# Decoder step on one core: the first pair of each down-projection part by seven products, with weight sums made ahead and kept in DRAM

## The chip, the cores and the metric

The kernel runs on one core of one Trainium2 chip. The metric is the device time of one execution in microseconds (us), given as the median of the runs; lower is better. Engines are named as in the profile: PE (matrix products), DVE (elementwise work), ACT (copies, casts, activations), POOL (elementwise work and its own DMA queue) and SP (which only issues DMAs). The profile is one execution taken by the hardware profiler.

## What is computed

One layer of a decoder for 512 prompt tokens and 8 sample tokens (520 columns), D = 2048, feed-forward width 5632, in float32:

```
h = h + W_out [ GatedDeltaNet(x_n) ; MultiScalePool(x_n) ]    x_n = RMSNorm(h)
gu = RMSNorm(h) @ w_gate_up                                   # 2048 -> 2 x 5632
h = h + (silu(gu[..., :D_FF]) * gu[..., D_FF:]) @ w_down      # 5632 -> 2048
y = RMSNorm(h)
```

Only the last two products, gate/up and down, matter for this change. The result must hold to float32 accuracy, so that every operand is cut into a high part `hi` (float32r, a rounded copy) and a rest `lo` = x - hi, and a product of two 128-row tiles is three matmuls: hi x hi, hi x lo, lo x hi.

## The kernel before, in words

**Pairs and products.** The work of gate/up and down is tiled in pairs (class `Pair`): a pair makes two 128-row output tiles for all 520 columns. Its weight is a 2 x 2 block matrix (A11, A12, A21, A22: two output tiles by two halves of the contraction), its input a 2 x 2 block matrix (B11, B21 for the first 260 columns, B12, B22 for the last 260). Each block product is 8 tiles of the contraction deep in gate/up, and 7, 7 or 8 in down; each depth is three matmuls of 260 columns (`passes`, L1265 to L1270). Done plainly a pair takes eight block products (`plain`, L1324). Most pairs go by Strassen's scheme in the form of Winograd (`strassen`, L1401): seven products M1 to M7, on the weights A11, A12, A22 and four sums S1 to S4 of them, and on the inputs B11, B21, B22 and four sums T1 to T4. The sums of the inputs are shared by all pairs of a stage; the sums of the weights are made anew for each pair (`add`, L1284, one DVE operation each) and then cut (`cut_raw`: an ACT cast to hi at L1261, a DVE subtraction to lo at L1262).

**Look-ahead.** In `strassen` a weight is added up or cut three to four products before PE reads it. Three rotating buffers (`wpl`) and one extra take the cut weights in turn, so that a cut waits for the product four places earlier. Products go into five PSUM banks; `combine` (L1307) empties them on DVE, most of it after M6.

**Parts of down.** The contraction of down (44 tiles) is done in three parts (`SIZES = (7, 7, 8)` pairs of tiles). The inputs of a part are the eight quarters that gate/up wrote to DRAM (`a_d`, by `to_dram` on POOL). At the start of a part all seven forms (B11, B21, B22, T1 to T4, each with a hi and a lo tile in SBUF) change over while PE goes on: `cross` runs the last pair of the part before by eight plain products, then the first pair of the new part by eight plain products too, because plain pairs read only B11, B21, T1 and B22. In between, `fill` brings each form in: `fetch` loads it from `a_d` in pieces of two tiles into staging rows (POOL's DMA queue; free rows in the first part, seven rotating `st` buffers later), ACT cuts it to hi (L1831) and DVE to lo (L1832). The order of all this is written by hand in the tables `TAIL`, `LAST` and `HEAD`, whose entries are carried out at fixed steps of the two plain pairs. There are three such crossings, one for each part.

**Queues.** Weights are loaded by SP (L1253), forms and rows of h by POOL, each in program order. In gate/up a hook (`hidden`) is called ahead of each product and places other work there: the gating of each tile pair, and the recurrent state of the sample tokens (on POOL).

## Time and profile before

| | |
|---|---|
| median of 3 runs (lowest to highest) | 2152.28 us (2151.39 to 2152.33) |
| the profiled execution, its own time | 2151.82 us |
| its span | 2150.1 us |
| mean granted PE clock | 0.999 |
| PE busy | 2123.7 us, 17746 matmuls |
| DVE busy | 1757.6 us, 2629 instructions |
| ACT busy | 929.3 us |
| POOL busy | 490.9 us |
| moved by DMA | 305.44 MB |

Times in the profile are counted from the start of the span. A group line gives line, engine, operation, output and inputs, shape and count; then the busy time of the group in us and the mean of one in ns; then the idle time of its engine just ahead of it and who ended it. A timeline row gives start, duration, engine, line, operation, and in brackets the idle time ahead of it with its releaser. The window view gives for each stretch its length, the busy time of each engine with the count of its instructions, the granted PE clock, the share of time that the 16 DMA engines were busy, and the GB/s that they moved.

Gate/up's Strassen pairs run from about 820 to 1650 us, the three crossings lie near 1650, 1800 and 1945 us, and the span ends with the output stage from 2130 us.

### The profile page before, as it was taken

The numbers are of one execution on the slowest core, as the hardware profiler recorded it, in microseconds if no ns is written. First come the engines' busy times: TensorE is split into PE (matmuls) and PEld (weight loads), VectorE is DVE, ScalarE is ACT, GpSimd is POOL, SyncE is SP. The second block draws the span as 40 slices with busy tenths as digits, with TensorE's granted clock in tenths as the row PEclk, the third lists the DMA queues.
The fourth block names the chain that finished last, engine by engine and source line by source line (L and its number), as shares of the span: only waits on it lengthen the run. The fifth ranks groups of instructions, "written<-read, shape, count | busy, mean of one in ns | idle before, by whom it ended". The sixth has DMA issues, their size and how long they took to land.

```text
span 2150.1 us, 43041 instructions
## 1 busy us (share of the span) xinstructions
PE 2123.7 (99%) x17746; PEld 2110.5 (98%) x17746; DVE 1757.6 (82%) x2629; ACT 929.3 (43%) x1404; POOL 490.9 (23%) x602
## 2 busy tenths in 40 slices
PE   8999999999999999999999999999999999999998
PEld 7999999999999999999999999999999999999998
DVE  7786767666599979988888888888887897887997
ACT  6533442433255454434434434434434444435444
POOL 3212320222012202333333333331113302003100
PEclk9999999999999999999999999999999999999999
DMA  8344434434445534455455455454456746438333
GB/s 282 90 119 114 117 104 113 116 111 107 129 134 160 158 99 132 144 163 148 141 165 148 138 168 148 135 171 134 119 148 197 226 112 205 115 104 250 91 108 119
DMA packets 445826, 305.44 MB, mean 142 GB/s; under 512 B 27836, under 2 KB 424533, under 8 KB 442285
## 3 DMA queue, kind: packets, MB, share of 16 engines
q1 hardware_dynamic: 422733, 219.94, 36.6%
q0 software_dynamic: 21584, 81.95, 12.0%
q8 instruction: 139, 2.28, 0.4%
q10 hardware_dynamic: 1312, 0.80, 0.1%
q14 instruction: 58, 0.48, 0.1%
HBM read 255.66 MB, written 47.63 MB: 141 GB/s over the span
## 4 chain that ended last, share of the span: by engine, by line
PE 85%; DVE 8%; DMA 2%; issue 2%; ACT 1%; POOL 1%; DVEq 0%; SPq 0%; ACTq 0%; POOLq 0%
PE dn L1269 21%; PE dn L1268 21%; PE dn L1270 21%; PE mm L168 5%; PE mm L170 5%; PE mm L169 5%; DVE lo L1262 1%; DVE lo L137 1%; PE dn L870 1%; DMA st<-a_d 1%; DMA qk<-tok_d 1%; PE mm L1268 1%; PE mm L1269 0%; DVE raw L1290 0%; PE mm L1270 0%
## 5 line engine op out<-in xcount | busy, mean ns | idle before, releaser
L1262 DVE TENSOR_TENSOR lo<-raw,hi 128x1024 fp32r<-128x1024 f32 (+1 forms) x422 | 530.6, 1277 | 87.0 <-ACT hi L1261 85.5
L1261 ACT CAST hi<-raw 128x1024 fp32r<-128x1024 f32 (+1 forms) x422 | 427.5, 1027 | 403.1 <-DVE raw L1290 205.4
L168 PE MATMUL mm<-xh,hi 128*128 128x256 f32 (+1 forms) x1280 | 376.4, 294 | 3.1 <-DVE mixa L259 3.1
L169 PE MATMUL mm<-xl,hi 128*128 128x256 f32 (+1 forms) x1280 | 361.6, 283 | 0.9 <-DVE xl L350 0.7
L170 PE MATMUL mm<-xh,lo 128*128 128x256 f32 (+1 forms) x1280 | 361.7, 283 | 0.4 <-DVE lo L137 0.4
L168 PEld LDWEIGHTS mm<-xh,hi 128*128 128x128 f32 x1280 | 241.2, 188 | 7.1 <-DVE mixa L259 3.8
L169 PEld LDWEIGHTS mm<-xl,hi 128*128 128x128 f32 x1280 | 241.6, 189 | 1.7 <-DVE xl L350 1.7
L170 PEld LDWEIGHTS mm<-xh,lo 128*128 128x128 f32 x1280 | 240.9, 188 | 0.6 <-DVE lo L137 0.6
L1290 DVE TENSOR_TENSOR raw<-raw 128x1024 f32<-128x1024 f32 (+1 forms) x130 | 175.1, 1347 | 2.2
L1269 PE MATMUL dn<-b21l,hi 128*128 128x260 f32 x620 | 175.7, 283 | 0.1
L1270 PE MATMUL dn<-b21h,lo 128*128 128x260 f32 x620 | 175.4, 283 | 0.0
L1268 PE MATMUL dn<-b21h,hi 128*128 128x260 f32 x620 | 174.9, 282 | 0.0
L1270 PE MATMUL dn<-b11h,lo 128*128 128x260 f32 x612 | 173.2, 283 | 1.3 <-DVE lo L1262 1.3
L1269 PE MATMUL dn<-b11l,hi 128*128 128x260 f32 x612 | 173.3, 283 | 0.0
L1268 PE MATMUL dn<-b11h,hi 128*128 128x260 f32 x612 | 172.8, 282 | 0.0
L1454 POOL TENSOR_TENSOR mixa<-mixa 128x520 f32<-128x520 f32 x22 | 51.3, 2333 | 493.0 <-DVE mixa L1448 493.0
L1268 PE MATMUL dn<-T1h,hi 128*128 128x260 f32 x556 | 158.1, 284 | 0.0
L1269 PE MATMUL dn<-T1l,hi 128*128 128x260 f32 x556 | 157.7, 284 | 0.0
L1270 PE MATMUL dn<-T1h,lo 128*128 128x260 f32 x556 | 156.8, 282 | 0.0
L1268 PE MATMUL dn<-B22h,hi 128*128 128x260 f32 x548 | 155.9, 284 | 0.0
L1269 PE MATMUL dn<-B22l,hi 128*128 128x260 f32 x548 | 155.6, 284 | 0.0
L1270 PE MATMUL dn<-B22h,lo 128*128 128x260 f32 x548 | 154.6, 282 | 0.4 <-DVE lo L1262 0.4
(669 smaller groups left out, 6480.7 us busy)
## 6 DMA issues: line engine op xcount, KB each, us to landing
raw<-in_w_gate_up_dram SPq DMA_DIRECT2D x134, 512.0 KB
raw<-in_w_in_dram SPq DMA_DIRECT2D x79, 512.0 KB
a_d<-mixa POOLq DMA_DIRECT2D x22, 1040.0 KB, 5.5
raw<-in_w_down_dram SPq DMA_DIRECT2D x48, 448.0 KB
mixb<-in_w_gate_up_dram SPq DMA_DIRECT2D x41, 512.0 KB
raw<-in_w_out_dram SPq DMA_DIRECT2D x25, 512.0 KB
st<-a_d POOLq DMA_DIRECT2D x49, 260.0 KB, 6.6
raw<-in_w_down_dram SPq DMA_DIRECT2D x24, 512.0 KB
```

What stands on the lines that cost most here:

```text
L137: dve.tensor_tensor(lo[:, r], raw[:, r], hi[:, r].bitcast(F32), op=ALU.subtract)
L168: te.matmul(acc[ci], wh, hi[k][:, c0:c1], start=(k == 0), stop=False)
L169: te.matmul(acc[ci], wh, lo[k][:, c0:c1], start=False, stop=False)
L170: te.matmul(acc[ci], wl, hi[k][:, c0:c1], start=False, stop=(k == len(w) - 1))
L870: te.matmul(yp[0:96, c, j], xt_[:, c, :], udf[:, c, j] if it == 0 else v3(cur)[:, c, j], start=True, stop=True)
L1261: act.copy(hi, raw)
L1262: dve.tensor_tensor(lo, raw, hi.bitcast(F32), op=ALU.subtract)
L1268: te.matmul(acc, wh[:, k, :], xf[:, k, :], start=start and k == 0, stop=False)
L1269: te.matmul(acc, wh[:, k, :], xg[:, k, :], start=False, stop=False)
L1270: te.matmul(acc, wl[:, k, :], xf[:, k, :], start=False, stop=stop and k == wh.shape[1] - 1)
L1290: dve.tensor_tensor(r[name], r[a], r[b], op=op)
L1454: pool.tensor_tensor(q[:, 4:8:2, :], q[:, 1:4:2, :], q[:, 0:2, :], op=ALU.subtract)
```

## The change

The first pair of each part of down is computed by the seven products instead of eight. Its weight sums S1 to S4, cut into hi and lo, are made during gate/up and stored to DRAM (`sums_d`); at the crossing they are loaded back as they are. The forms are loaded straight into their own lo tiles and cut in place there, so that the staging rows go. For each of the three first pairs:

- in gate/up, `sums_ahead` is a generator of twelve steps, taken one per gate/up pair (ahead of product 5 of even pairs and of product 2 of odd ones): four loads of weight blocks, four sums and four lo cuts on DVE, four hi casts on ACT, and eight stores by SP;
- at the crossing, `recall` loads the eight tiles (SP), S1 to `xcp`, S2 to the pool "sg", S3 and S4 to the pool "sf"; A11, A12 and A22 are loaded and cut as before;
- the first pair's products go in the order `CROSSED`, and it joins the run of the other pairs of its part.

```diff
+    CROSSED = ("M4", "M7", "M1", "M6", "M5", "M2", "M3")
...
-    rows = [mix[m] for m in (4, 5, 10, 11, 12, 13, 14, 15)]
+    sums_d = dram.tile([len(SIZES), 4, 2, P, HG * P], F32, name="sums_d")
...
+        def recall(self, name, pool_):
+
+            src, n = self.sums[int(name[1]) - 1], self.width
+            w = [pool_.tile([P, HG * P], F32R, tag=x, name=x)[:, :n] for x in ("hi", "lo")]
+            for j, t in enumerate(w):
+                sp.dma_start(t.bitcast(F32), src[j, :, :n])
+            self.w[name] = [t.rearrange("p (k c) -> p k c", c=P) for t in w]
...
-        steps = [(q, n) for q in range(len(pairs)) for n in (order if q == len(pairs) - 1 else STEADY)]
+        steps = [(q, n) for q in range(len(pairs)) for n in (
+            CROSSED if pairs[q].sums is not None else order if q == len(pairs) - 1 else STEADY)]
...
+            if p4 and p4.sums is not None and name4[0] == "S":
+                name4 = ""
+            if p and p.sums is not None and name[0] == "S":
+                name = ""
...
     def fetch(name, part_):
 
-        n = SIZES[part_]
-        staged[name] = []
+        n, fp = SIZES[part_], sum(SIZES[:part_])
         for r in range(0, n, 2):
             k = min(2, n - r)
-            if part_ == 0:
-                st = rows[len(spare) % len(rows)]
-                spare.append(name)
-            else:
-                st = stage[-1][1].tile([P, NTOK], F32, tag="st", name="st", bufs=7)
...
+            pool.dma_start(forms[name][1][:, r:r + k, :].bitcast(F32),
+                           a_d[fp + r:fp + r + k, :, QUARTER.index(name), :].rearrange("k p c -> p k c"))
 
     def fill(name, part_):
...
         hi, lo = forms[name]
...
+        for r in range(0, SIZES[part_], 2):
+            x = slice(r, min(r + 2, SIZES[part_]))
+            raw = lo[:, x, :].bitcast(F32)
+            act.copy(hi[:, x, :], raw)
+            dve.tensor_tensor(lo[:, x, :], raw, hi[:, x, :].bitcast(F32), op=ALU.subtract)
...
-    LAST = {0: ("+A11", "+A21", "+A12", "T3"), 1: ("+A22", "B11"), 2: ("A11",), 3: ("T1", "A21"), 4: ("A12", "B21", "<B22")}
-    HEAD = {0: ("B22", "+A11", "+A22", "+A21"), 1: ("+A12",), 2: ("A11", "S3", "T2"), 3: ("A22",), 4: ("-S3", "S2")}
+    LAST = {0: ("<B11", "T3"), 1: ("+A12", "?S1"), 2: ("<T1", "A22", "T2"), 3: ("<B21", "A11", "B11"), 4: ("<B22", "T1")}
+    CROSS = {2: ("?S4", "B21"), 3: ("B22",)}
...
-    def cross(part_, last, done=None, then=None):
-
-        r21, r21_ = r21s if part_ == 0 else r21s[1:] * 2
+    def cross(part_, last):
+
+        first = dps[part_][0]
+        for x in ("T4", "T3", "T2"):
+            fetch(x, part_)
         last.cut("A12")
-        fill("T4", part_)
-        last.plain(lambda step: turn(LAST[step], dps[part_][0], r21, part_))
...
-        dps[part_][0].plain(lambda step: turn(HEAD[step], dps[part_][1], r21_, part_))
...
+        turn(("+A22", "?S3", "+A11", "?S2", "T4"), first, part_)
+        last.plain(lambda step: turn(LAST[step], first, part_))
...
     def hidden(q, j):
...
+        if j == (1 if q % 2 else 4):
+            next(ahead, None)
...
-        run(dps[part_ - 1][1:-1], r21s[1], None, STEADY, dps[part_ - 1][-1])
+        run(dps[part_ - 1][:-1], r21s[1], None, STEADY, dps[part_ - 1][-1], part_ - 1)
         cross(part_, dps[part_ - 1][-1])
```

In these tables `+` loads a weight block, `?` recalls a stored sum, `<` only fetches a form, a weight's bare name cuts it, and a form's bare name fills it. `LAST` is read at steps of the plain last pair (step 0 stands behind product 2, 1 behind 4, 2 behind 5, 3 behind 7, 4 behind 8), `CROSS` ahead of products 3 and 4 of the first pair.

**DVE in gate/up**, from the first sum of M6 of an early gate pair on, before:

```order
L1313 TENSOR_TENSOR cm<-cm,dn 128x260
L1314 TENSOR_TENSOR cm<-cm,dn 128x260
L1434 TENSOR_TENSOR sg<-cm,dn 128x260
L1262 TENSOR_TENSOR lo<-raw,hi 128x1024 x2
L1434 TENSOR_TENSOR sg<-cm,dn 128x260
```

and now, where L1262 has become L1263, L1313 and L1314 are L1323 and L1324, the gate's sums are L1451, and L1962 is a sum of `sums_ahead`:

```order
L1323 TENSOR_TENSOR cm<-cm,dn 128x260
L1324 TENSOR_TENSOR cm<-cm,dn 128x260
L1451 TENSOR_TENSOR sg<-cm,dn 128x260
L1263 TENSOR_TENSOR lo<-raw,hi 128x1024
L1962 TENSOR_TENSOR mixb<-mixb 128x896
L1263 TENSOR_TENSOR lo<-raw,hi 128x1024
```

One sum has come in between the cut of this pair's S4 and that of the next pair's A11, which stood next to each other.

**SP at the first crossing**, from the first load of a down weight, before (the number behind a name tells one buffer from another; the blocks are A11, A21, A12 and A22 of the first pair, then A11, A22, A21 and A12 of the second, and A21 of the third):

```order
L1253 DMA raw_19774<-in_w_down_dram 128x7x128
L1253 DMA mixb_99<-in_w_down_dram 128x7x128
L1253 DMA raw_19777<-in_w_down_dram 128x7x128
L1253 DMA raw_19845<-in_w_down_dram 128x7x128
L1253 DMA raw_20056<-in_w_down_dram 128x7x128
L1253 DMA raw_20058<-in_w_down_dram 128x7x128
L1253 DMA sg_9697<-in_w_down_dram 128x7x128
L1253 DMA raw_20109<-in_w_down_dram 128x7x128
L1253 DMA sg_9697<-in_w_down_dram 128x7x128
```

and now (A22; S3; A11; S2; A12; S1; A21 of the second pair; S4):

```order
L1254 DMA raw_19796<-in_w_down_dram 128x7x128
L1291 DMA hi_19798<-sums_d_7807 128x896
L1291 DMA lo_19799<-sums_d_7807 128x896
L1254 DMA raw_19802<-in_w_down_dram 128x7x128
L1291 DMA hi_19804<-sums_d_7807 128x896
L1291 DMA lo_19805<-sums_d_7807 128x896
L1254 DMA raw_19935<-in_w_down_dram 128x7x128
L1291 DMA hi_19937<-sums_d_7807 128x896
L1291 DMA lo_19938<-sums_d_7807 128x896
L1254 DMA sg_9698<-in_w_down_dram 128x7x128
L1291 DMA hi_20150<-sums_d_7807 128x896
L1291 DMA lo_20151<-sums_d_7807 128x896
```

Eight loads of stored sums have come in between the weight loads. The last two, S4, stand ahead of the loads of the second pair's A11, A22 and A12.

**DVE at the second crossing**, from the cut of the first pair's A12 on, before (`st` is a staging row, `b21` the tile of B21; L1867 and L1868 add a product to a row of h, the last plain product of the old part):

```order
L1262 TENSOR_TENSOR lo<-raw,hi 128x896
L1832 TENSOR_TENSOR b21l<-st,b21h 128x520 x3
L1832 TENSOR_TENSOR b21l<-st,b21h 128x260
L1867 TENSOR_TENSOR mixa<-mixa,cm 128x260
L1868 TENSOR_TENSOR mixa<-mixa,dn 128x260
L1832 TENSOR_TENSOR B22l<-st,B22h 128x520 x3
```

and now, from the fill of T1 to that of B21 (L1839 is L1832, L1874 and L1875 are L1867 and L1868):

```order
L1839 TENSOR_TENSOR T1l<-T1l,T1h 128x520 x3
L1839 TENSOR_TENSOR T1l<-T1l,T1h 128x260
L1874 TENSOR_TENSOR mixa<-mixa,cm 128x260
L1875 TENSOR_TENSOR mixa<-mixa,dn 128x260
L1839 TENSOR_TENSOR b21l<-b21l,b21h 128x520 x3
L1839 TENSOR_TENSOR b21l<-b21l,b21h 128x260
```

The adds of the last plain product stood between the fills of B21 and B22; now they stand right behind the fill of T1 and ahead of that of B21, and each fill reads the form's own lo tile.

124 lines of the change are left out of this document (85 added, 39 removed).

## Prediction

> **What bounds the kernel now.** I read the page first, then the stretches between, then single rows.
>
> ```profile
> span 2150.1 us, 43041 instructions
> ...
> PE 2123.7 (99%) x17746; PEld 2110.5 (98%) x17746; DVE 1757.6 (82%) x2629; ACT 929.3 (43%) x1404; POOL 490.9 (23%) x602
> ...
> PE 85%; DVE 8%; DMA 2%; issue 2%; ACT 1%; POOL 1%; DVEq 0%; SPq 0%; ACTq 0%; POOLq 0%
> ```
>
> PE is busy nearly all of the span, and the chain that ended last runs through PE for 85% of it. An average does not say where; the stretches that the change touches do:
>
> ```profile
> core 0: us, PE busy (x) PEld busy (x) DVE busy (x) ACT busy (x) POOL busy (x), PEclk, DMA share, GB/s
> 900.00:1000.00 100.00, 100.00 (x833) 100.00 (x832) 85.87 (x91) 39.48 (x49) 33.23 (x26) 1.00 0.50 148
> 1400.00:1500.00 100.00, 100.00 (x833) 100.00 (x832) 85.71 (x93) 41.28 (x52) 26.38 (x21) 1.00 0.51 150
> 1799.00:1841.00 42.00, 42.00 (x352) 42.00 (x351) 32.53 (x55) 23.97 (x41) 17.92 (x27) 1.00 0.84 254
> 1990.00:2130.00 140.00, 140.00 (x1165) 140.00 (x1164) 129.77 (x165) 69.14 (x84) 10.92 (x7) 1.00 0.33 91
> ```
>
> In gate/up (first two), in the second crossing (third) and in the last part of down (fourth) PE is never idle, at full clock. So a matmul taken out of these stretches shortens the span by its pace, if nothing new makes PE wait. DVE is the engine next to full, with 14 of 100 us free in gate/up. In the crossing it is DMA, at 0.84.
>
> The pace of a matmul is not the duration of its record. It comes from DVE's first sum after M6, which waits for PE in each pair:
>
> ```profile
> 1219.81 0.43 DVE L1313 TENSOR_TENSOR cm<-cm,dn 128x260 f32<-128x260 f32 x1 [1.12 <-PE dn L1270]
> ...
> 1240.04 0.42 DVE L1313 TENSOR_TENSOR cm<-cm,dn 128x260 f32<-128x260 f32 x1 [1.29 <-PE dn L1270]
> ...
> 1777.65 0.43 DVE L1313 TENSOR_TENSOR cm<-cm,dn 128x260 f32<-128x260 f32 x1 [1.64 <-PE dn L1270]
> ...
> 1795.34 0.43 DVE L1313 TENSOR_TENSOR cm<-cm,dn 128x260 f32<-128x260 f32 x1 [1.64 <-PE dn L1270]
> ```
>
> A pair of gate/up is seven products of 8 x 3 matmuls: 20.23 us / 168 = 0.1204 us. A pair of a seven-tile part of down is 17.69 us / 147 = 0.1203 us. So a product takes 2.53 us in parts one and two, and 2.89 us in part three and in gate/up.
>
> **The change, part by part: the product.** Each first pair loses one product of eight: 21 + 21 + 24 = 66 matmuls, 66 x 0.1204 = 7.95 us off PE. Taken by the record's mean
>
> ```profile
> L1268 PE MATMUL dn<-b21h,hi 128*128 128x260 f32 x620 | 174.9, 282 | 0.0
> ```
>
> it would be 66 x 0.282 = 18.6 us; but the records overlap (833 in 100 us), so that figure is no saving. The Trainium skill ("TensorE: Matmul & The Clock Gate", the section "Wait — 56ns, not 53.3ns?") gives a warm matmul N / 2.4 GHz plus about 2.5 ns, an estimate of 0.111 us for 260 columns and of 7.3 us for the 66. The trace's pace is 8% slower than that; the measured one is used.
>
> **Sums in gate/up.** Twenty-four DVE operations are added in 36 pairs: per part four sums and four lo cuts, one to a pair at most. The nearest rows for their kinds:
>
> ```profile
> L1290 DVE TENSOR_TENSOR raw<-raw 128x1024 f32<-128x1024 f32 (+1 forms) x130 | 175.1, 1347 | 2.2
> L1262 DVE TENSOR_TENSOR lo<-raw,hi 128x1024 fp32r<-128x1024 f32 (+1 forms) x422 | 530.6, 1277 | 87.0 <-ACT hi L1261 85.5
> L1290 DVE TENSOR_TENSOR sg<-raw,sg 128x896 f32<-128x896 f32 (+1 forms) x18 | 20.3, 1129 | 0.0
> L1262 DVE TENSOR_TENSOR lo<-sg,hi 128x896 fp32r<-128x896 f32 (+1 forms) x25 | 28.5, 1141 | 3.0 <-ACT hi L1261 2.6
> ```
>
> 16 of 896 columns at 1.13 and 8 of 1024 at 1.31 make 28.6 us of DVE over 36 x 20.23 = 728 us. That raises DVE from 86% to 90% there. What counts is whether one operation of 1.1 to 1.3 us makes a cut late:
>
> ```profile
> 1017.54 0.43 DVE L1313 TENSOR_TENSOR cm<-cm,dn 128x260 f32<-128x260 f32 x1 [0.20 <-PE dn L1270]
> ...
> 1221.13 2.35 DVE L1262 TENSOR_TENSOR lo<-raw,hi 128x1024 fp32r<-128x1024 f32 x2
> ```
>
> The second row is the cut of S4 and of the next pair's A11, done at 1223.48. M6 ended just ahead of 1219.81, and A11 is read after M5, M2 and M3, three products or 8.67 us later: a margin of 5.0 us, of which the inserted sum takes 1.1. S4 itself is cut ahead of it, at 1222.3, and read two products (5.78 us) after M6: a margin of 3.3 us, untouched. The lead is won back by the wait for M6, 1.1 to 1.3 us in the pairs shown ahead and 0.20 in the first row here, the shortest once the lead is built up. So I take the cost as nothing, with two covers: the margin of 3 to 5 us and then the wait. Without the covers it is 28.6 us. The twelve casts go to ACT, 40% busy there, and read sums finished a pair earlier. The twelve loads and 24 stores by SP (17.3 MB over 728 us, 24 GB/s on 148) take their inputs from the pair before, so SP does not stop in front of its weight loads for long.
>
> At the start of gate/up's pairs DVE is behind already, and the first sum falls there (ahead of the second pair's product 2):
>
> ```profile
> 841.27 0.39 PE L1270 MATMUL dn<-B22h,lo 128*128 128x260 f32 x1 [0.43 <-DVE lo L1262]
> ...
> 850.24 5.43 DVE L1262 TENSOR_TENSOR lo<-raw,hi 128x1024 fp32r<-128x1024 f32 x3
> ```
>
> PE idled 0.43 us for DVE at 841, and three cuts took 5.43 us a little later. One operation of 1.13 us here may cost PE from 0 to 1.1 us; I take 0.3, nearer to nothing, since from 900 us on PE does not stop.
>
> **The crossings.** Per crossing 8 x 448 KB of sums come back by SP in place of one block, 3.2 MB more (3.7 in the last). DVE's work hardly changes: one cut less, three adds of 0.42 us more. What is new is that a form can be loaded only when PE is done with its tile, where staging rows let the loads run ahead. T4, T3 and T2 are free before the plain pair begins. T1 is the tight one, because the adds of the last plain product stand behind its fill on DVE, and M6 of the first pair needs the PSUM bank that they empty:
>
> ```profile
> L1822 POOL DMA_DIRECT2D st<-a_d x56: 579/707/727, 1798.0 to 1979.0; - x56
> ...
> L1831 ACT CAST T1h<-st x8: 410/622/632, 1819.0 to 1969.2; 128x520 fp32r<-128x520 f32 x7, 128x260 fp32r<-128x260 f32 x1
> L1832 DVE TENSOR_TENSOR T1l<-st,T1h x8: 423/694/702, 1820.7 to 1969.9; 128x520 fp32r<-128x520 f32 x7, 128x260 fp32r<-128x260 f32 x1
> ...
> DMA to landing us min/median/max: 4.2/6.5/8.5
> ...
> L1867 DVE TENSOR_TENSOR mixa<-mixa,cm 128x260 f32<-128x260 f32 x44 | 18.6, 424 | 0.3
> L1868 DVE TENSOR_TENSOR mixa<-mixa,dn 128x260 f32<-128x260 f32 x44 | 18.7, 425 | 3.3 <-PE dn L1270 0.4
> ```
>
> Counted from the start of the second crossing's plain pair: T1 is free after five products, 12.6 us; four issues of 0.71 bring it to 15.5; landing takes 6.5 (at worst 8.5); the last piece is cast and subtracted in 0.83, the two adds take 0.85: 23.7 (25.7). M6 starts after eleven products, at 27.8. The margin is 4.1 (2.1) us, and more in the other two crossings, where products take longer. Behind a fetch that waits stand only the next fetches on POOL's queue; behind a cast that waits for its landing stand, on ACT, the casts of B21 and of the second pair, and on DVE their subtractions.
>
> S4's buffer is that of S3, so SP waits for M7, ten products or 25.3 us after the start, and behind SP's wait stand the second pair's A11, A22 and A12. M3 reads S4 at 35.4: 10.1 us for 2 x 448 KB. The nearest rows are three weight loads of 512 KB in gate/up:
>
> ```profile
> 1216.32 6.42 SPq L1253 DMA_DIRECT2D raw<-in_w_gate_up_dram  x3
> ...
> 1223.04 1.05 ACT L1261 CAST hi<-raw 128x1024 fp32r<-128x1024 f32 x1 [1.56 <-DMA raw<-in_w_gate_up_dram]
> ```
>
> The second had landed 6.7 us after the first was issued, with DMA at 0.5; that leaves 3.4 us. A11, 448 KB behind S4, lands some 2 to 3 us later and is wanted 15 products after the start, 37.9 us. I take 0.2 us for each crossing, 0.6 in all; the bounds are below.
>
> One wait at the third crossing goes with the old order:
>
> ```profile
> 1975.20 0.28 PE L1268 MATMUL dn<-b21h,hi 128*128 128x260 f32 x1
> 1975.54 0.39 PE L1269 MATMUL dn<-b21l,hi 128*128 128x260 f32 x1
> ```
>
> The step is 0.34 in place of 0.12: B21's fill came late by 0.2 us, as the first pair's third product. Now B21 is read by the sixth, so 0.2 us is gained. The tail keeps its order.
>
> **The sum.** -7.95 - 0.2 + 0.3 + 0.6 = -7.25 us on the profiled execution (2151.82 us; 1.72 outside the span): 2144.6. The median of the runs, 2152.28, is 0.46 above it: 2145.0.
>
> **The rivals.**
> *The crossings give some back.* Traffic of 42 us x 254 GB/s = 10.7 MB plus 3.2 is 13.9 MB in 39.5 us, where 254 / 0.84 = 302 GB/s at a full share move 11.9. The surplus of 2.0 MB is 6.5 us a crossing, if all lands within it; but T4, T3 and T2 (2.8 MB) are fetched during the Strassen pair ahead, which brings it to 11.1 MB, just below. So the bounds are 0 and 6.5 us; at 1 to 4 us each in place of 0.2, 2147.4 to 2156.4. For it speaks the thin rest, against it the margins of 2 to 4 us above. The Trainium skill ("DMA: Bandwidth & Descriptors", the section "Specifications") puts one core's share of memory at about 358 GB/s; by that 14.1 MB would fit and nothing be lost, but the rows' 302 is used.
> *Slower: the crossings are full.* Were the surplus paid whole, three times 6.5 is 19.5 us in place of my 0.6, and the time 2163.9. It turns slower than before from 2.6 us a crossing on (7.95 + 0.2 - 0.3 = 7.85, by three).
> *DVE falls behind in gate/up.* If the waits for M6 are no true spare, part of the 28.6 us shows on PE: 0.2 us in each of the 36 pairs takes back 7 us (2152); half of it 14 us (2159). The 14% of free time and the margins speak against it.
> *The saving is 18.6 us*, by the record's duration: 2134. The count of 833 per 100 us speaks against it.
>
> **Chances.** The forecast 0.74. The crossings give some back 0.14, of which 0.04 stay below 2148.0. Full crossings 0.04. DVE 0.06, half of it slower. 18.6 us 0.02. About 0.2% (4.3 us) is what a measurement can tell from no change: below 2148.0 is faster, 0.74 + 0.04 + 0.02 = 0.80; above 2156.6 slower, 0.04 + 0.03 = 0.07; the rest, 0.10 + 0.03 = 0.13, the same. The range: at the low end no stall at all and the wait gone, 2152.28 - 8.15, less 0.7, most of the 0.9 by which the runs spread, 2143.4; at the high end it takes in the crossings with 1.5 us each, 2148.9.
>
> **What would show it.** Right: 66 matmuls fewer, PE busy in every stretch of gate/up as before while DVE rises to about 90%, and the three crossings shorter by one product each. Wrong: PE waiting at a crossing for DVE's adds behind T1 (M6), for S4 (M3) or for the second pair's A11; DVE's wait for M6 gone over a row of gate/up pairs, with PE's count per 100 us below 833.

## The result, and the profile after

| kernel | median us | lowest to highest | runs |
|---|---|---|---|
| before | 2151.87 | 2151.39 to 2152.33 | 9 |
| changed | 2157.43 | 2152.34 to 2159.73 | 9 |

The ratio of the changed kernel to the one before is 1.0022, with a 95% interval of 1.0012 to 1.0033: slower by 5.6 us at the medians, where 7 us less was forecast. The runs also spread over 7.4 us where they had spread over 0.9. In the sessions of the experiments below the kernel before spread over 3.2 to 4.7 us itself, two runs far above (2682 and 7343 us) left aside.

The profiled execution of the changed kernel is the shortest of its nine (2152.34), which must be kept in mind below: it shows where the saving went, but not the whole loss of a median run. The top of its page:

```profile
span 2150.5 us, 43052 instructions
...
PE 2119.6 (99%) x17680; PEld 2104.8 (98%) x17680; DVE 1782.9 (83%) x2659; ACT 935.0 (43%) x1410; POOL 503.7 (23%) x602
...
PE 79%; DVE 10%; DMA 5%; issue 3%; ACT 2%; POOL 1%; SPq 0%; DVEq 0%; ACTq 0%; POOLq 0%
```

PE has its 66 matmuls fewer (17746 to 17680). But the chain that ended last now runs through PE for 79% instead of 85%, and through DMA for 5% instead of 2%. Transfers have come onto the path. The stretches say where:

```profile
core 0: us, PE busy (x) PEld busy (x) DVE busy (x) ACT busy (x) POOL busy (x), PEclk, DMA share, GB/s
900.00:1000.00 100.00, 100.00 (x833) 100.00 (x832) 90.16 (x96) 41.08 (x50) 36.03 (x26) 1.00 0.56 171
1400.00:1500.00 100.00, 100.00 (x832) 100.00 (x832) 87.99 (x95) 43.77 (x55) 30.85 (x24) 1.00 0.57 178
1650.00:1690.00 40.00, 40.00 (x334) 40.00 (x333) 29.95 (x46) 21.21 (x40) 22.50 (x33) 1.00 1.05 351
1690.00:1700.00 10.00, 7.98 (x55) 7.55 (x55) 4.40 (x7) 2.78 (x3) 3.77 (x7) 0.88 1.05 370
...
1945.00:1955.00 10.00, 7.91 (x63) 7.48 (x63) 4.79 (x9) 4.37 (x7) 0.00 (x0) 1.00 0.86 248
```

Gate/up (first two rows) is as forecast: DVE at 88 to 90% where it had 86%, PE at 833 and 832 matmuls per 100 us as before. The crossings are not. DMA is full at the first one (share 1.05, 351 to 370 GB/s), where the kernel before had 0.91 and 283 GB/s over the same 40 us; over 40 us from 1797 and from 1945 us on the share is 1.01 and 1.00, before 0.85 and 0.95. Around 1695 and 1950 PE loses 2 of 10 us. Around 1695 the granted clock is below full as well (0.88).

Single rows of the changed kernel, from the timelines of its engines, in order of time (start, duration, engine, what; in brackets the idle time before and what ended it):

```profile
825.13 0.39 PE L1271 MATMUL dn<-T4h,lo 128*128 128x260 f32 x1 [1.06 <-DVE lo L1263]
...
1644.42 0.43 DVE L1323 TENSOR_TENSOR cm<-cm,dn 128x260 f32<-128x260 f32 x1 [1.30 <-PE dn L1271]
...
1682.35 7.05 SPq L1254 DMA_DIRECT2D raw<-in_w_down_dram  x3
...
1684.02 1.08 POOL L2124 DMA_DIRECT2D mixa<-h_d  x2
1685.09 2.65 POOL L2124 DMA_DIRECT2D mixb<-h_d  x5
...
1694.37 0.94 ACT L1262 CAST hi<-raw 128x896 fp32r<-128x896 f32 x1 [8.23 <-DMA raw<-in_w_down_dram]
...
1695.36 0.39 PE L1269 MATMUL dn<-b11h,hi 128*128 128x260 f32 x1 [1.40 <-ACT hi L1262]
...
1696.49 0.39 PE L1271 MATMUL dn<-b11h,lo 128*128 128x260 f32 x1 [0.62 <-DVE lo L1263]
...
1697.55 0.42 PE L1270 MATMUL dn<-b11l,hi 128*128 128x260 f32 x1
...
1934.71 2.86 POOL L1830 DMA_DIRECT2D T4l<-a_d  x4 [107.75 <-PE dn L1270]
...
1937.66 14.26 SPq L1254 DMA_DIRECT2D raw<-in_w_down_dram  x4
...
1949.46 0.94 ACT L1262 CAST hi<-raw 128x896 fp32r<-128x896 f32 x1 [8.64 <-DMA raw<-in_w_down_dram]
...
1950.45 0.39 PE L1269 MATMUL dn<-b11h,hi 128*128 128x260 f32 x1 [1.47 <-ACT hi L1262]
...
1951.58 0.39 PE L1271 MATMUL dn<-b11h,lo 128*128 128x260 f32 x1 [0.62 <-DVE lo L1263]
...
2144.12 0.34 ACTq L2094 DMA_DIRECT2D out_dram<-os  x1
```

Two weights come late. *At the first crossing* it is A11 of the second pair. SP issues it at 1682.35 (the first of x3), its cast starts at 1694.37, 12.0 us later, and PE waits 1.40 us for hi and 0.62 us for lo. Two us after the issue POOL puts seven residual rows (`h_d`, 260 KB each) onto the same DMA engines. *At the third crossing* it is A11 of the last pair, the one that runs plainly. SP issues it at 1937.66, but POOL has begun to fetch T4, T3 and T2 at 1934.71; the cast starts 11.8 us after the issue, and PE waits 1.47 + 0.62 us. The second crossing has the same wait, 0.41 us (at 1804.94). In the kernel before, the same places look like this:

```profile
826.15 0.39 PE L1270 MATMUL dn<-T4h,lo 128*128 128x260 f32 x1 [1.04 <-DVE lo L1262]
...
1644.57 0.42 DVE L1313 TENSOR_TENSOR cm<-cm,dn 128x260 f32<-128x260 f32 x1 [1.29 <-PE dn L1270]
...
1689.04 0.94 ACT L1261 CAST hi<-raw 128x896 fp32r<-128x896 f32 x1 [1.58 <-PE dn L1269]
...
1693.03 1.14 POOL L2047 DMA_DIRECT2D mixa<-h_d  x2 [5.87 <-DVE T2l L1832]
...
1938.48 8.78 SPq L1253 DMA_DIRECT2D raw<-in_w_down_dram  x4
...
1942.74 0.94 ACT L1261 CAST hi<-raw 128x896 fp32r<-128x896 f32 x1 [1.11 <-DMA raw<-in_w_down_dram]
...
1944.53 4.95 POOL L1822 DMA_DIRECT2D st<-a_d  x7 [113.22 <-PE dn L1270]
...
2144.57 0.35 ACTq L2030 DMA_DIRECT2D out_dram<-os  x1
```

There POOL's waits had put things in order, unasked. The rows went out at 1693, behind the fills of the staging tiles, when the second pair's A11 was being cast already (1689.04). The fetches went out at 1944.5, when the staging tiles opened, after the last pair's A11 had been cast (1942.74, 4.3 us after its issue).

The two profiled executions, cut at the rows above (first wait of gate/up, M6 of its last pair, issue of the last output write, end):

| stretch | before | changed | difference |
|---|---|---|---|
| start to the first wait of gate/up | 826.15 | 825.13 | -1.02 |
| gate/up from there to its last M6 | 818.42 | 819.29 | +0.87 |
| crossings and down, to the last write's issue | 500.00 | 499.70 | -0.30 |
| from there to the end of the span | 5.53 | 6.38 | +0.85 |

In the third stretch 7.95 us should have gone, and 0.30 went: 7.65 us were lost there. I call this number "lost" in what follows: the stretch from the last M6 of gate/up to the last write's issue, less 500.00, plus 7.95.

### The profile page after: what moved, and what is told of

Its sections match the earlier page's. It is cut to its first block, busy times and chain, and to the rows that moved or that the text cites. A ratio compares the mean times of both kernels' runs of the same rounds, so it can differ in the third digit from the quotient of the medians.

```text
span 2150.5 us, 43052 instructions
## 1 busy us (share of the span) xinstructions
PE 2119.6 (99%) x17680; PEld 2104.8 (98%) x17680; DVE 1782.9 (83%) x2659; ACT 935.0 (43%) x1410; POOL 503.7 (23%) x602
## 4 chain that ended last, share of the span: by engine, by line
PE 79%; DVE 10%; DMA 5%; issue 3%; ACT 2%; POOL 1%; SPq 0%; DVEq 0%; ACTq 0%; POOLq 0%
PE dn L1269 19%; PE dn L1271 19%; PE dn L1270 19%; PE mm L168 5%; PE mm L170 5%; PE mm L169 5%; DVE lo L1263 2%; DMA raw<-in_w_down_dram 2%; DVE raw L1300 1%; DVE lo L137 1%; DMA raw<-in_w_gate_up_dram 1%; ACT hi L1262 1%; PE dn L870 1%; DMA qk<-tok_d 1%; PE mm L1269 1%
## 5 line engine op out<-in xcount | busy, mean ns | idle before, releaser
L1262 ACT CAST hi<-raw 128x1024 fp32r<-128x1024 f32 (+1 forms) x422 | 427.7, 1027 | 455.1 <-DVE raw L1300 254.1
L1263 DVE TENSOR_TENSOR lo<-raw,hi 128x1024 fp32r<-128x1024 f32 (+1 forms) x422 | 536.3, 1288 | 99.3 <-ACT hi L1262 97.7
L1270 PE MATMUL dn<-b21l,hi 128*128 128x260 f32 x598 | 169.4, 283 | 0.0
L1471 POOL TENSOR_TENSOR mixa<-mixa 128x520 f32<-128x520 f32 x22 | 59.1, 2686 | 470.7 <-DVE mixa L1465 470.7
L1271 PE MATMUL dn<-b21h,lo 128*128 128x260 f32 x598 | 169.2, 283 | 0.0
L1269 PE MATMUL dn<-b21h,hi 128*128 128x260 f32 x598 | 168.7, 282 | 0.0
L1269 PE MATMUL dn<-T1h,hi 128*128 128x260 f32 x534 | 151.9, 284 | 0.0
L1270 PE MATMUL dn<-T1l,hi 128*128 128x260 f32 x534 | 151.5, 284 | 0.0
L1271 PE MATMUL dn<-T1h,lo 128*128 128x260 f32 x534 | 150.6, 282 | 0.0
L1269 PE MATMUL dn<-B22h,hi 128*128 128x260 f32 x526 | 149.6, 284 | 0.0
L1270 PE MATMUL dn<-B22l,hi 128*128 128x260 f32 x526 | 149.4, 284 | 0.0
L1271 PE MATMUL dn<-B22h,lo 128*128 128x260 f32 x526 | 148.4, 282 | 0.4 <-DVE lo L1263 0.4
```

The source lines that it names most:

```text
L1262: act.copy(hi, raw)
L1263: dve.tensor_tensor(lo, raw, hi.bitcast(F32), op=ALU.subtract)
L1269: te.matmul(acc, wh[:, k, :], xf[:, k, :], start=start and k == 0, stop=False)
L1270: te.matmul(acc, wh[:, k, :], xg[:, k, :], start=False, stop=False)
L1271: te.matmul(acc, wl[:, k, :], xf[:, k, :], start=False, stop=stop and k == wh.shape[1] - 1)
L1471: pool.tensor_tensor(q[:, 4:8:2, :], q[:, 1:4:2, :], q[:, 0:2, :], op=ALU.subtract)
```

## The experiments

**My theory** after this reading: (1) the early fetches of T4, T3 and T2 and the row loads run ahead of weights that PE needs first; (2) a pause of PE above some length is followed by a stretch at half clock, and since the pause at the first crossing differs from run to run, this gives the spread. **Rivals**: the added work in gate/up costs the time; the clock drops for another reason; it is the total traffic of the crossings that is too much, and not its order.

All times below are medians, and the ratio is to the kernel before in the same session, with its 95% interval. The changed kernel's 2157.43 is from the first session, with 2151.87 for the kernel before; in the later sessions that has medians of 2151.4 to 2151.9, so that times can be compared across them to about half a us. "Lost" is of the one profiled execution, from its two rows as above.

| kernel | median us | ratio [95%] | profiled run us | last M6, last write | lost us |
|---|---|---|---|---|---|
| changed | 2157.43 | 1.0022 [1.0012, 1.0033] | 2152.34 | 1644.42, 2144.12 | 7.65 |
| e1 sums in gate/up only | 2151.85 | 1.0000 [0.9991, 1.0009] | 2153.04 | | |
| e2 T2 fetched first | 2154.82 | 1.0016 [1.0007, 1.0025] | 2157.70 | 1645.09, 2149.39 | 12.25 |
| e3 rows by SP | 2150.01 | 0.9993 [0.9984, 1.0003] | 2150.26 | 1643.36, 2141.87 | 6.46 |
| e4 S4 behind A11 | 2154.13 | 1.0021 [1.0012, 1.0030] | 2157.54 | 1643.52, 2149.31 | 13.74 |
| e5 changed, again | 2154.72 | one run | 2154.72 | 1643.34, 2146.51 | 11.12 |
| e7 one tile per sum | 2151.37 | 0.9994 [0.9985, 1.0003] | 2147.11 | 1643.38, 2138.91 | 3.48 |
| e8 e3 + e7 | 2150.58 | 0.9997 [0.9988, 1.0006] | 2150.58 | 1643.41, 2142.27 | 6.81 |
| e9 e3 + T3 first | 2150.39 | 0.9997 [0.9988, 1.0006] | 2152.72 | 1643.75, 2144.53 | 8.73 |
| e10 e3 + one tile for S3, S2, S1 | 2152.46 | 1.0006 [0.9998, 1.0015] | 2150.38 | 1644.88, 2141.93 | 5.00 |
| e11 e9 + e10 | 2153.59 | 1.0012 [1.0003, 1.0021] | 2153.36 | 1643.37, 2144.86 | 9.44 |
| e12 e3 + T2 first | 2150.65 | 0.9994 [0.9985, 1.0003] | 2149.12 | 1644.62, 2140.64 | 3.97 |
| e13 e12 + S4 behind A11 | 2147.79 | 0.9981 [0.9972, 0.9990] | 2148.89 | 1644.05, 2140.50 | 4.40 |
| e14 e8 + T2 first | 2152.62 | 1.0002 [0.9993, 1.0011] | 2153.84 | 1644.33, 2145.16 | 8.78 |

### Gate/up by itself (e1)

The sums are made and stored in gate/up as in the changed kernel, and nothing reads them; the rest is the kernel before.

```diff
     def hidden(q, j):
...
+        if j == (1 if q % 2 else 4):
+            next(ahead, None)
```

> The kernel before, with only the gate/up part of the change added: the weight sums of the three first pairs are made, split and stored to DRAM as in the changed kernel, but nothing reads them and the first pairs stay plain. My theory (the time is lost at the crossings): 2152 to 2153.5 us, about 0.9 us over the kernel before, mean clock 0.999 as before. Rival 1 (the extra DVE operations in gate/up cost the time): the changed kernel is at 2157.4 with 7.95 us saved, so the cost of 13.5 us should show here: about 2165, at least 2160. Rival 2 (the clock is lowered by the added work in gate/up, whatever PE's waits): about 2156, with a mean clock of 0.997.

Measured: 2151.85, no difference from before. A stretch of gate/up in its profile:

```profile
900.00:1000.00 100.00, 100.00 (x832) 100.00 (x832) 89.98 (x96) 41.25 (x50) 34.32 (x25) 1.00 0.56 169
```

DVE is at 90% and DMA at 0.56, as in the changed kernel, and PE keeps its 832. The rivals that put the loss into gate/up fall: the margins of 3 to 5 us and the wait for M6 did cover the added work.

### The order of the early fetches (e2)

```diff
-        for x in ("T4", "T3", "T2"):
+        for x in ("T2", "T3", "T4"):
             fetch(x, part_)
...
-        turn(("+A22", "?S3", "+A11", "?S2", "T4"), first, part_)
+        turn(("+A22", "?S3", "+A11", "?S2", "T2"), first, part_)
...
-    LAST = {... 2: ("<T1", "A22", "T2"), ...
+    LAST = {... 2: ("<T1", "A22", "T4"), ...
```

> The changed kernel with one order turned round: at each crossing T2 is fetched first, then T3, then T4 (and T2 is filled first, T4 last of the three). POOL's queue then waits for the fourth product of the Strassen pair ahead and not for the second, so that the last pair's A11 is issued some 2 us ahead of all fetches in place of 3 us behind the first. My theory (the early fetches delay the last pair's A11): the A11 of crossings two and three lands in 4 to 7 us in place of 11.7, the stalls of 0.7 and 2.6 us there go, and so does the clock loss that follows them: 2150 to 2154 us, against 2157.4 unchanged. Rivals (gate/up, or a clock that drops for another reason): 2156 to 2158, no change, with the stalls gone or not.

Measured: 2154.82, 2.6 us below the changed kernel and 0.8 above the range expected. Rows of its timelines:

```profile
1700.71 0.59 PE L1269 MATMUL dn<-b11h,hi 128*128 128x260 f32 x1 [6.09 <-ACT hi L1262]
...
1943.09 9.15 SPq L1254 DMA_DIRECT2D raw<-in_w_down_dram  x4
...
1947.71 0.94 ACT L1262 CAST hi<-raw 128x896 fp32r<-128x896 f32 x1 [1.47 <-DMA raw<-in_w_down_dram]
```

At the third crossing the mechanism is as the theory has it: the last pair's A11 lands in time again (cast 4.6 us after its issue, 11.8 before), and PE's waits in the last pairs of crossings two and three are gone. A part of it comes back later in the third crossing, as a wait for the recalled S1 (0.76, at 1987.11) and in the second pair (1.14, at 2006.50). And the first crossing, which this edit doesn't help, shows in this run what the first profile had hidden: PE waits 6.09 us for the second pair's A11.

### The residual rows (e3), and the place of S4 (e4)

```diff
-    for mp in ORDER[1:]:
-        for m in (2 * mp, 2 * mp + 1):
-            pool.dma_start(mix[m], h_d[m])
+    def rows_later(q, j):
+        if j == 5:
+            for mp in {0: ORDER[1:2], 1: ORDER[2:4]}.get(q, ORDER[q + 2:q + 3]):
+                sp.dma_start(mix[2 * mp], h_d[2 * mp])
+                sp.dma_start(mix[2 * mp + 1], h_d[2 * mp + 1])
```

> The changed kernel with one transfer moved: the 14 row loads of the residual (h_d, 3.7 MB) that POOL issues all at once during the first Strassen pair of part one are issued by SP instead, two to four per pair, over the first six pairs. My theory (at the first crossing the rows share the DMA engines with the second pair's A11, which takes 11.9 us to land): the stall of 2.55 us at 1695 us and the half clock of 3.4 us behind it go; 2152 to 2155 us against 2157.4. Rival (A11 is late because it stands behind S4 on SP and behind the recalls, not because of the rows): the A11 still lands about 10 us after its issue, and the time stays at 2156 to 2158.

```diff
-    CROSS = {2: ("?S4", "B21"), 3: ("B22",)}
+    CROSS = {2: ("B21",), 3: ("?S4", "B22")}
```

> The changed kernel with one order turned round on SP at each crossing: the second pair's A11 is issued ahead of the recall of S4 (which waits for M7, because it takes S3's buffer) and not behind it. If A11 is late because of its place behind S4, it is issued 1 to 3 us earlier, has 0.9 MB less ahead of it, the stall of 2.55 us at the first crossing shrinks to 0 to 1 us, S4 still arrives in time for M3, and the time is 2153 to 2156. If it is late because of the row loads that share the DMA engines, the stall stays above 1.5 us and the time at 2156 to 2158; a new wait for S4 ahead of M3 would make it longer.

Measured: e3 at 2150.01, 7.4 us below the changed kernel, more than was expected. e4 at 2154.13. Rows of e3:

```profile
1681.30 5.60 SPq L1254 DMA_DIRECT2D raw<-in_w_down_dram  x3
...
1690.62 0.95 ACT L1262 CAST hi<-raw 128x896 fp32r<-128x896 f32 x1 [5.55 <-DMA raw<-in_w_down_dram]
...
1946.78 0.39 PE L1269 MATMUL dn<-b11h,hi 128*128 128x260 f32 x1 [2.45 <-ACT hi L1262]
```

And of e4:

```profile
1686.23 0.95 ACT L1262 CAST hi<-raw 128x896 fp32r<-128x896 f32 x1 [1.00 <-DMA raw<-in_w_down_dram]
...
1699.88 0.94 ACT L1262 CAST hi<-raw 128x896 fp32r<-128x896 f32 x1 [12.71 <-DMA raw<-in_w_down_dram]
...
1700.87 0.58 PE L1269 MATMUL dn<-T4h,hi 128*128 128x260 f32 x1 [5.30 <-ACT hi L1262]
```

With the rows out of the way A11 is cast 9.3 us after its issue instead of 12.0, and PE doesn't wait for it at the first crossing; the third keeps its wait (2.45 us here, with 3.4 us of half clock behind it), and the runs of e3 spread over 8.7 us. With S4 behind A11 but the rows still there, A11 is cast at 1686 and is no trouble, but the next weight, A22, is the victim: PE waits 5.30 us for it ahead of T4's product. The expectation of e4 had not named this case. So at the first crossing the rows cost the time, and a change of order in front of them only picks who pays. The larger part of A11's 12.0 us is not theirs, though: 9.3 us are left without them (e3), and 7.2 us when A11 goes ahead of S4 (e4, issued at 1679.01).

### The changed kernel once more (e5), and the price of a pause (e6)

> The changed kernel unchanged, one more execution with its profile. Eight of its nine runs took 2155.4 to 2159.7 us, at mean clocks of 0.996 to 0.998, and only the profiled one 2152.3 at 0.999. My theory (the second pair's A11 at the first crossing lands later in most executions, so that PE's pause there is longer, and a stretch at half clock follows it) expects in a run of 2156 to 2159 us a pause of 4 to 7 us near 1695 us and a half-clock stretch behind it, gate/up as in the first profile. Rival (a clock that is lowered elsewhere): the pause at 1695 stays near 2.5 us, and stretches below full clock stand away from any pause.

It took 2154.72 us. Rows at the first crossing:

```profile
1696.11 0.39 PE L1269 MATMUL dn<-b11h,hi 128*128 128x260 f32 x1 [3.23 <-ACT hi L1262]
...
1697.24 0.58 PE L1271 MATMUL dn<-b11h,lo 128*128 128x260 f32 x1 [0.59 <-DVE lo L1263]
```

The run is 2.4 us longer than the first profiled one and has 3.23 + 0.59 us of waiting at this place where that had 1.40 + 0.62, and behind it 24 matmuls at half pace where that had 15. The pause is a little below the 4 to 7 us expected, as is the time.

For the price, the kernel before got extra DVE work in twelve pairs of gate/up, where DMA is far from full:

```diff
+        if j == 4 and q >= 4 and q % 3 == 1 and q < 40:
+            for _ in range((5, 6, 7, 8, 10, 12)[q // 3 % 6]):
+                dve.tensor_tensor(slow[0], slow[0], slow[1], op=ALU.add)
```

> The kernel before with DVE operations put in on purpose in twelve pairs of gate/up (5, 6, 7, 8, 10 and 12 of 1.2 to 1.35 us each, that sequence twice, just ahead of the cut of the next pair's A11), so that PE has to wait there: pauses from about 1 to about 10 us by the margin of 5 us that the prediction gave. Theory (a pause of more than about 1.5 us is followed by a stretch at half clock): behind the pauses of 2 us and more the matmuls come at 0.24 us in place of 0.12 for 3 to 6 us, 1.5 to 3 us more than the pause itself costs; behind those of 1 us nothing. Rival (a pause costs its own length, and the half clock at the first crossing has another cause): full clock behind all twelve.

One run, 2254.53 us, 102.8 above before. PE's twelve waits are 1.00, 1.01, 3.53 (twice), 5.29, 6.10, 7.30, 7.31, 8.62 (twice), 11.28 and 13.67 us. Stretches of 6 us behind one of 1 us and one of 3.53 us:

```profile
1280.30:1286.30 6.00, 5.95 (x49) 5.95 (x50) 6.00 (x9) 2.38 (x3) 0.00 (x0) 1.00 0.00 0
1413.30:1419.30 6.00, 5.99 (x27) 6.00 (x28) 6.00 (x9) 2.37 (x3) 0.00 (x0) 0.50 0.02 3
```

And the rows at those places:

```profile
1280.35 0.39 PE L1270 MATMUL dn<-b11h,lo 128*128 128x260 f32 x1 [1.00 <-DVE lo L1262]
...
1413.31 0.58 PE L1270 MATMUL dn<-b11h,lo 128*128 128x260 f32 x1 [3.53 <-DVE lo L1262]
1413.69 0.42 PE L1268 MATMUL dn<-b11h,hi 128*128 128x260 f32 x1
...
1418.89 0.42 PE L1268 MATMUL dn<-T4h,hi 128*128 128x260 f32 x1
```

Behind 1 us of waiting PE goes on at full clock, 49 matmuls in 6 us. Behind 3.53 us it does 27, at a granted clock of 0.50. All ten waits of 3.5 us and more are followed by such a stretch, 2.9 to 6.2 us long from PE's first matmul on (4.6 in the mean); neither of the two of 1 us is. The waits add up to 77.3 us; the other 25.5 us are 2.5 us for each of the ten, of which half clock over 4.6 us explains 2.1 (a matmul comes every 0.217 us there, not every 0.120). So the second part of the theory holds for long pauses, and it needs no DMA: here DVE made them. The Trainium skill ("TensorE: Matmul & The Clock Gate", the section "HAM oscillation — how this bites in real kernels") gives the rule that no gap of PE should exceed about 3.4 us. The ten waits agree; but in the changed kernel 1.40 + 0.62 us, 1.1 us apart, were enough once (1695, rows above), and nearly the same, 1.47 + 0.62, were not (1950).

The traces show a difference between the two places. In the changed kernel the granted clock first rises at 11.35 us, and falls and rises again at 1697.53 and 1700.95, which is 494 and 495 times 3.413 us later; in every trace here the changes lie on such a grid, counted from that run's own first rise (10.1 to 15.6 us after the start). Four stretches of the changed kernel's grid:

```profile
1694.12:1697.53 3.41, 1.55 (x10) 1.34 (x11) 2.09 (x4) 0.94 (x1) 2.50 (x5) 1.00 1.06 351
1697.53:1700.95 3.42, 3.42 (x18) 3.42 (x17) 3.16 (x6) 1.85 (x2) 1.18 (x3) 0.50 1.06 375
...
1946.71:1950.12 3.41, 2.27 (x19) 2.05 (x17) 0.00 (x0) 0.66 (x1) 0.00 (x0) 1.00 1.05 328
1950.12:1953.54 3.42, 2.47 (x18) 2.26 (x19) 3.00 (x5) 2.25 (x4) 0.00 (x0) 1.00 0.59 149
```

The first pause falls into one stretch, in which PE is busy for 1.55 of 3.41 us, and the next stretch is at half clock; the second pause is cut in two by the grid, 2.27 and 2.47 us remain busy, and the clock stays. So what counts seems to be how long PE is idle within one stretch, and the same pause can cost more or less by where it falls. This was read off afterwards and not tested, and it isn't a plain threshold: e9 drops to half behind stretches with 1.82 and 1.74 us busy, e10 keeps full clock behind one with 1.56.

### Fewer bytes (e7, e8, e10, e11)

Only the sum itself is stored and recalled, 1.8 to 2.1 MB less for each crossing, and it is cut at the crossing.

```diff
-            for j, t in enumerate(w):
-                sp.dma_start(t.bitcast(F32), src[j, :, :n])
+            sp.dma_start(w[1].bitcast(F32), src[0, :, :n])
...
+        def split(self, name):
+            hi, lo = self.w[name]
+            raw = lo.bitcast(F32)
+            act.copy(hi, raw)
+            dve.tensor_tensor(lo, raw, hi.bitcast(F32), op=ALU.subtract)
```

> The changed kernel with half the traffic of the sums: only the sum itself is stored and recalled, into the lo tile, and cut there at the crossing (one cast and one subtraction for each of four sums, 4.6 us of DVE at each crossing; S3 at step 2 of the plain pair, S2 at step 3, S1 at step 4, S4 in the fifth product of the first pair). Each crossing reads 1.8 to 2.1 MB less, 5 to 6 us at 350 GB/s. Theory (the crossings' transfers delay PE's weights): the pauses at the first crossing shrink by half or more, 2148 to 2154 us against 2157.4. Rival (it is the order of the early fetches and rows alone, or DVE at the crossing, that counts): 2156 or more.

> Both relief measures together: sums recalled as one tile each and cut at the crossing, and the residual rows loaded by SP over six pairs in place of at once by POOL. Theory: the first crossing has no pause left, the third keeps a part of the wait for the last pair's A11 (2.7 us in the kernel with the rows moved alone, at 2150.0): 2145 to 2149 us, below the kernel before by 3 to 7 us. Rival (something else than the crossings' transfers takes the saving): 2150 or more.

Measured: e7 2151.37, inside its range, 6.1 us below the changed kernel. But on top of e3 the smaller traffic brings nothing: e8 at 2150.58, e3 at 2150.01, where 2145 to 2149 was expected. Its profile has no wait of the second pair at the first crossing, but PE waits 1.08 us at the first crossing for the lo tile of S4, whose cut stands on a busy DVE, and still 1.99 + 0.63 us for the last pair's A11 at the third.

e10 takes S4 back to two tiles, e11 adds T3 first:

```diff
-            for j, t in enumerate(w):
+            for j, t in enumerate(w if name == "S4" else w[1:]):
```

> Rows moved to SP and three of the four sums (S3, S2, S1) stored and recalled as one tile and cut at the crossing; S4, whose cut cost PE 1.1 us at the first crossing and 0.2 to 0.4 at the others, is stored in two parts again. Against the same with S4 cut at the crossing too (2150.6): the waits for S4's lo tile go, 1.7 us in all, 2147 to 2150 us. If DVE at the crossings is what counts, three cuts more still show there as waits for lo tiles, and the time stays at 2150 or more.

> All three measures: rows by SP, S3, S2 and S1 as one tile each, fetches in the order T3, T4, T2. Theory: none of the waits above 1 us at the three crossings is left, no stretch at half clock, and of the 7.95 us saved some 6 to 7 remain: 2144.5 to 2147.5 us, with runs within 2 us of one another as in the kernel before. Rival (something else than the crossings' transfers takes the saving and spreads the runs): 2149 or more, with runs 5 us apart.

Both missed: 2152.46 and 2153.59. The wait for S4's cut is gone as expected, but the second pair's A11 is late again at the first crossing (1.86 + 0.61 us in e10, 1.93 + 0.61 in e11), although the rows are moved and fewer bytes run. SP issues it later there, 39.5 us behind the last M6 of gate/up in both, 37.9 in e3; why it then lands 10.9 us after its issue in e10, and after 9.3 us in e3, I can't tell from the traces. e11 also waits 0.89 + 0.62 us for a weight of the last pair at the third crossing, and behind both places come 3.4 us of half clock. What follows all the same: fewer bytes don't by themselves bring a weight in time.

### Later fetches (e9, e12, e13, e14)

```diff
-        for x in ("T4", "T3", "T2"):
+        for x in ("T3", "T4", "T2"):
             fetch(x, part_)
```

> The kernel with the residual rows moved to SP (2150.0), and the early fetches in the order T3, T4, T2, so that POOL's queue waits for the third product of the Strassen pair ahead instead of the second: 2.5 us later, about as the last pair's A11 is issued. Theory (the fetches ahead of that A11 delay it): it lands in 5 to 8 us in place of 11.7, the wait of 2.0 to 2.5 us at the third crossing goes or falls below 1 us: 2146 to 2149 us. Rival (the total traffic of the third crossing counts, and a wait only moves to another weight): 2149 to 2152, with a new wait between 1950 and 2005 us.

Measured: 2150.39, in the range of the rival (2149 to 2152, the wait moved to another weight) and not in the theory's. A11 of the last pair is in time, but its A12, two issues behind, is not; the second crossing has the same wait (0.97 + 0.62 us), and behind both come 3.4 us of half clock. Two rows of e9:

```profile
1953.82 0.94 ACT L1262 CAST hi<-raw 128x896 fp32r<-128x896 f32 x1 [8.14 <-DMA raw<-in_w_down_dram]
1954.81 0.39 PE L1269 MATMUL dn<-b21h,hi 128*128 128x260 f32 x1 [1.14 <-ACT hi L1262]
```

By the theory 2.5 us later is not late enough, and e12 starts the fetches later still. It is e3 with T2 first, e13 is e12 with S4 behind A11 (the edit of e4), e14 is e8 with T2 first.

> Rows moved to SP and the early fetches in the order T2, T3, T4, so that they start about 5 us later than in the changed kernel, behind the issue of all three of the last pair's late weights. With T3 first the wait only moved from that pair's A11 to its A12. Theory (order of service: what is issued ahead of the fetches lands in time): no wait in a last pair is left; the third crossing keeps the later waits of the same fetch order without the rows moved (0.8 us for S1, 1.1 us for T2's weight), and the first none above 0.5 us: 2147 to 2150 us. Rival (total traffic: what is put off by 5 us makes the later weights late at every crossing): new waits at crossings one and two as well, 2150 or more.

> As the kernel with rows moved and T2 first, and the second pair's A11 issued ahead of the recall of S4. With the rows out of the way A22, the weight behind S4, should no longer be the victim (it waited 5.3 us when only S4 was put behind). Theory (order): the first crossing is free of waits in more of the executions, and the runs spread less: 2146.5 to 2149 us. Rival (total traffic): A22 or S4 is late instead, and the time is the same as without this step, or above it.

> Rows moved to SP, T2 first, and all four sums stored and recalled as one tile each and cut at the crossing (1.8 to 2.1 MB less at each crossing). If total traffic makes the later weights late, this kernel has none of the waits for S1 and T2's weight at the third crossing and keeps only those for S4's cut (1.1, 0.2 and 0.4 us): 2145.5 to 2148 us, below the same without the halved recall. If order alone counts, the cuts cost as much as the traffic saves, and the two are within 1 us of one another.

Measured: e12 2150.65, just over its range, though its profiled run has only what was expected: nothing above 0.3 us at the first crossing, nothing at the second, 0.77 and 1.14 us at the third. e13 2147.79, runs from 2145.5 to 2149.0: faster than the kernel before by 0.2% (0.9981, interval 0.9972 to 0.9990), the only kernel here for which that is shown. Why it is 2.9 us below e12 the two profiles don't show, as both are free of waits above 0.3 us at the first crossing; the runs of e12 spread over 5.2 us, those of e13 over 3.5. e14 2152.62, so the smaller traffic adds 2 us to e12 instead of saving, which neither side had expected. The two longest waits left at the crossings in e13's profile, both at the third:

```profile
1972.51 0.36 PE L1269 MATMUL dn<-b11h,hi 128*128 128x260 f32 x1 [1.26 <-DVE mixa L1875]
...
1980.28 0.39 PE L1271 MATMUL dn<-T1h,lo 128*128 128x260 f32 x1 [0.77 <-DMA lo<-sums_d]
```

And the longest one in e14, at the same crossing:

```profile
1981.48 0.56 PE L1269 MATMUL dn<-T1h,hi 128*128 128x260 f32 x1 [3.11 <-DVE mixa L1880]
```

The first row of e13 and that of e14 are waits for a PSUM bank: the adds of the last plain pair (L1875, in e14 L1880) stand on DVE behind a cut and a fill, and these wait for a cast whose input lands late. In e13 that is the first pair's A11 (ACT idles 4.22 us for it, until 1966.81), in e14 the recalled S1, which has to be cut there ahead of T1's fill (5.91 us, until 1975.72); T1 itself had been fetched from 1957 to 1960. It is the kind of wait that the prediction looked for at M6, here at M1 (e13, on B11) and M5 (e14, on T1). In e14 it is the longest, with half clock behind it.

**What follows.** e13 moves every byte that the changed kernel moves and takes 9.6 us less, and from 1650 to 1690 us its DMA is just as full (share 1.06, 354 GB/s, against 1.05 and 351). From 1690 to 1700 us, when the second pair's first weights are due, it moves 139 GB/s where the changed kernel moves 370: most of the rows have gone to later pairs. So what runs just ahead of a due time decides more than the sum over the crossing. At the third crossing this is shown by order alone (e2: A11 from 11.8 to 4.6 us, with the same bytes); at the first, order alone was not enough (e4), and the rows had to leave. e8 and e14 move about 2 MB less at each crossing and gain nothing over the same order with all bytes, and only where the rows are still in the way (e7) do fewer bytes help; but these kernels pay with four cuts at the crossing that wait for their sums, so that none of them tests the bytes alone. The rival of total traffic thus falls as the main cause, but it isn't wholly out: in e2, e12 and e13 the third crossing (eight tiles to a part where the others have seven) keeps waits of about 1 us each. My first theory was too simple as well: e11, which it had below 2147.5, came out at 2153.6.

## Why the prediction was wrong, step by step

- **The product removed, -7.95: right.** 66 matmuls fewer, and 832 to 833 of them still pass in 100 us. Neither profile of the changed kernel shows a wait at the place of the old B21 wait, so the -0.2 holds as well.
- **Gate/up, +0.3: right.** e1 shows no cost; its stretch from the first wait to the last M6 (826.37 to 1644.84) is 0.05 us longer than before, the changed kernel's 0.87 in the first profile and 0.30 in e5 (824.62 to 1643.34). DVE at 90% was covered, as argued.
- **The margins of T1 (4.1 us) and S4 (3.4 us): they held.** PE waited for neither in the changed kernel.
- **The crossings, +0.6: wrong; this term sank the forecast.** It measured 7.65 us in one profile and 11.12 in the other (2.5 and 3.7 us per crossing), just about the 2.6 us from which the prediction had the change turn slower. The pauses account for it: from one matmul's start to the next, less the pace, the six waits of the first profile cost 5.7 us (0.16 us more each than the idle time in brackets), and the half clock 1.5; together 7.2 of the 7.65. Two steps of the term failed. The first: "T4, T3 and T2 (2.8 MB) are fetched during the Strassen pair ahead, which brings it to 11.1 MB, just below". It took the early fetch for relief. A sum of bytes over a window has no due times in it; in that very pair SP loads the last pair's weights one after the other, each just ahead of its use, and these come behind the fetches (4.3 us from issue to cast before, 11.8 after). The second: "A11, 448 KB behind S4, lands some 2 to 3 us later". It was cast 12.0 us after its issue and 13.2 us after that of S4 (1681.22), where the prediction's reckoning gives 8.7 to 9.7. The 14 row loads (3.7 MB) were in no sum and in no list of queues, though they were in the program: removing the staging tiles removed POOL's wait at 1693 that had held them back. e3 shows their price, 7.4 us at the median.
- **The rate of 302 GB/s** (254 at a share of 0.84) was too low: a full share carried 351 over 40 us and up to 370. The 358 GB/s of the Trainium skill ("DMA: Bandwidth & Descriptors", the section "Specifications"), which the prediction set beside it, are near the 351; the 370 over 10 us lie above. By such a rate the 13.9 MB that the prediction counted fit. At the first crossing the uncounted 3.7 MB of rows come on top; at the third, without rows, time was lost none the less.
- **What a wait costs** was taken as its length. Behind the pauses at the first crossing came half clock: 15 matmuls at 0.217 us instead of 0.120 in the first profile (1.5 us), 24 in e5 (2.3 us).
- **The end of the span** was taken as unchanged. The last output write is issued 0.45 us earlier and the span ends 0.4 us later. In every kernel built on the change this last piece is 6.4 to 6.9 us, in the kernel before, e1 and e6 about 5.5. So about 0.9 us of the saving is given back behind the last write's issue. The list of DMA queues from 2137 us to the end has one line in the changed kernel that the kernel before lacks:

```profile
q8 instruction: 1, 0.02, 0.4%
```

This is one packet of 16 KB that takes 0.95 us, 2.7 us ahead of the last write's issue. All thirteen traces with the long piece have it there, and the three with the short one don't. The output writes then end 5.0 us behind that issue instead of 3.8, and in their last us (2148.1 to 2149.1) the DMA share is 0.06, one engine of 16. That this packet holds that engine up is argued from this, not shown.
- **The rivals.** The one that "the crossings give some back", with 1 to 4 us each, was the case that came, a little beyond its upper end (2156.4); 0.14 was too little for it. DVE in gate/up and the saving of 18.6 us did not come.

What stays open: a median run of the changed kernel (2157.4) is 5 us longer than the profiled one, and was itself not profiled. That these 5 us are longer pauses at the first crossing, with more half clock behind them, is borne out by e5 (2154.7) and by e2 (6.09 us, in a run of 2157.7). The mean granted clocks of the nine runs point the same way: 0.999 in the profiled one and 0.996 to 0.998 in the others, which is roughly 4 to 13 us more at half clock, or 2 to 6 us of time. The spread says less: it is 3.5 us in e13, but 3.2 in the kernel before in that session, and 8.7 in e3, where the first crossing of the profiled run is clean. For the median run the cause is argued, not shown. What decides between a pause of 1.4 and one of 6 us at the same place of the same program was not tried.

## What to carry to other kernels

When a change takes away a buffer, look for what its waits had held back: a transfer that may start earlier will, and it competes with what has the nearest due time. Beside the sum of bytes over a window, list for each weight its issue, what is on the DMA engines just then, and its due time; a wait on an issuing queue is a tool for keeping that order. A pause of PE of some 1.5 us or more may cost 1.5 to 2.5 us beyond its length.
